# A two-layer decoder trunk on one core: the first chunk's inputs and weight pieces loaded and traced by turns, with identity products ahead of the data

## The chip, the cores and the metric

The kernel runs on one core of a Trainium2 chip. TensorE (PE in the profile) multiplies matrices, VectorE (DVE) and ScalarE (ACT) work element by element, GpSimd (POOL) does a few small operations, and SyncE (SP) issues the loads. Each engine has its own row of instructions and waits for others through semaphores. The metric is the time of one execution on the device in microseconds; a smaller number is better.

## The reference

An input of 256 tokens by 1024 channels goes through two layers. Each layer is a half-step SwiGLU feed-forward network, a token mixer (a causal convolution module in the first layer, a gated linear recurrence in the second) and another half-step feed-forward network, each between two RMS norms. The change lies in the very first feed-forward network:

```python
def rms_norm(x, gain):
    x32 = x.astype(jnp.float32)
    y = x32 * lax.rsqrt(jnp.mean(x32 * x32, axis=-1, keepdims=True) + EPS)
    return (y * gain.astype(jnp.float32)).astype(x.dtype)

def swiglu_ffn(x, w_in, w_out):
    gate, up = jnp.split(x @ w_in, 2, axis=-1)
    return (jax.nn.silu(gate) * up) @ w_out
...
    for layer in range(DEPTH):
        g = norm_gains[layer]
        h = swiglu_ffn(rms_norm(x, g[0]), ffn_w_in[layer, 0], ffn_w_out[layer, 0])
        x = x + 0.5 * rms_norm(h, g[1])
```

## The kernel before

The 256 tokens are two tiles of 128 (`xs[0]`, `xs[1]`). Every float32 operand is split into a high part (a cast on ACT, names `wh`, `xth`, `hid`) and a low part, the rest (a subtraction on DVE, names `wl`, `xtl`), and every product is three matmuls: high by high, high by low, low by high.

Weights come as pieces of 128 x 1024 floats, 512 KB each. `weight()` issues the load on SP into one of 4 `raw` buffers, and `split` makes `wh` on ACT and `wl` on DVE, of which there are 10 buffers each. With `fine` a piece is split in two halves. SP issues in order, and a load waits until DVE has read the piece that had its buffer. A chunk of a feed-forward network has 4 pieces of the first matrix and 2 of the second; a network has 11 chunks.

`pre_norm` transposes a tile of the input with the identity matrix on PE (L168), four blocks at a time into a `tr` buffer, scales them into `xth` on ACT (L172) and makes `xtl` on DVE (L178). In the first network `start` traces: tile 0's `pre_norm`, the four first pieces (`first_weights`), tile 1's `pre_norm`, then the means of squares (L156). `project_both` multiplies the first chunk for both tiles, 48 matmuls of 512 columns. `up` applies the gate to its result (L316 on ACT, L318 and L320 on DVE), and `turn` transposes that on PE (L189); from the second chunk on `channels` (L281 to L283) makes the products and `down` the second matrix (`acc`).

A scheduler orders each engine's instructions when the program is built. `tc.issue_after(i)` adds only this: what is traced inside stands behind `i` on `i`'s own engine. Behind chunk 2 `constants` is traced: `tap_spectrum` loads `dft` and the convolution's taps `w_dw` (31 rows of 4 KB), splits both, and multiplies them into `tr` buffers (the 31-row matmuls); `lower_bound` loads `logits`, `gnorm` and `masks`, and DVE casts the masks (L683).

Of the kernel before, what the change touches and what calls it, by code (L numbers as in the profile page):

```python
# [16 lines left out]
P = 128  # L17
# [23 lines left out]
def trunk_kernel(  # L41
# [62 lines left out]
    nc.sync.dma_start(xs[0][:, :512], x_in[0, :P, :512])  # L104
    nc.sync.dma_start(gcol, cols)
    nc.sync.dma_start(xs[0][:, 512:], x_in[0, :P, 512:])
    nc.sync.dma_start(xs[1], x_in[0, P:, :])
# [4 lines left out]
    last_hi = [None]  # L112
    last_split = [None]

    def weight(fine=False, eng=dve):
# [3 lines left out]
        nc.sync.dma_start(src, wts[n, :, half * 1024 : half * 1024 + 1024])  # L119
# [3 lines left out]
        with ExitStack() as held:  # L123
            if stream[0] <= 4:
                held.enter_context(tc.issue_after(last_hi[0]))
            for a in range(0, 1024, step):
                split(hi[:, a : a + step], lo[:, a : a + step], src[:, a : a + step], eng)
        return hi, lo

    def split(dst_h, dst_l, src, eng=dve):  # L130
        last_split[0] = act.copy(dst_h, src).ins  # L131
        eng.tensor_tensor(dst_l, src, dst_h.bitcast(F32), op=ALU.subtract)  # L132

    def mm3(o, lh, ll, rh, rl, first, last):
        pe.matmul(o, lh, rh, start=first, stop=False)  # L135
        pe.matmul(o, lh, rl, start=False, stop=False)  # L136
        pe.matmul(o, ll, rh, start=False, stop=last)  # L137
# [23 lines left out]
    def pre_norm(t, gi):  # L161
        src = xs[t]
        hi, lo = xth[:, t * D : (t + 1) * D], xtl[:, t * D : (t + 1) * D]
        for h in range(2):
            pt = tr()
            for j in range(4):
                k = h * 4 + j
                pe.transpose(pt[:, j * P : (j + 1) * P], src[:, k * P : (k + 1) * P], ident)  # L168
            for j in range(4):
                k = h * 4 + j  # L170
                g = gcol[:, gi * KD + k : gi * KD + k + 1]
                last_hi[0] = act.activation(hi[:, k * P : (k + 1) * P],  # L172
                                            pt[:, j * P : (j + 1) * P], AF.Copy, scale=g).ins
            for j in range(4):
                k = h * 4 + j
                g = gcol[:, gi * KD + k : gi * KD + k + 1]
                sl = slice(k * P, (k + 1) * P)
                dve.scalar_tensor_tensor(  # L178
                    lo[:, sl], pt[:, j * P : (j + 1) * P], g, hi[:, sl].bitcast(F32),
                    op0=ALU.mult, op1=ALU.subtract,  # L180
                )
# [648 lines left out]
```

## Time and profile before

| what | value |
|---|---|
| time, median of 3 runs | 1042.51 us (1040.93 to 1042.89) |
| span of the profiled execution, the only time the page gives of it | 1041.2 us |
| PE busy | 1011.2 us, 97% of the span |
| DVE busy | 707.1 us, 68% |
| ACT busy | 505.3 us, 49% |
| DMA, mean over the span | 174 GB/s |

The span runs from the first to the last instruction. A busy share is the part of the span in which an engine had an instruction running; the 3% in which PE did not are the places to look at.

### The profile page before, as it was taken

Reading aid. Unit: us, or ns where it says so; the run is one execution under the profiler, and the core shown is the slowest. Engines: PE = TensorE matmul, PEld = TensorE weight load, DVE = VectorE, ACT = ScalarE, POOL = GpSimd, SP = SyncE. Lnnn points to the kernel's source line nnn. Section 1 sums busy time; section 2 is a strip of 40 time slices with the busy share of each in tenths; the row PEclk is TensorE's granted clock in tenths of the full one; section 3 lists DMA queues with packets and bytes.
Section 4 is the critical chain, followed back from the end, with each engine's and each line's share of the span. In section 5 each row is a group of like instructions: output and inputs, shape, how many; then the busy total and the mean of one; then the engine's idle time right before and its main releaser. Section 6 shows DMA issues by size and latency. Waiting matters only on the chain. (4 is left out here: it accounts for less than half of the span.)

```text
span 1041.2 us, 16859 instructions
## 1 busy us (share of the span) xinstructions
PE 1011.2 (97%) x6676; PEld 920.0 (88%) x6676; DVE 707.1 (68%) x1088; ACT 505.3 (49%) x852; POOL 77.1 (7%) x120
## 2 busy tenths in 40 slices
PE   7989999999799999999999999999999999999997
PEld 6979999978678999999899999979888879999996
DVE  6845656699887657567856666686777686566663
ACT  7554444573575444445644445474133474444441
POOL 1000000010211000000100000021343010000000
PEclk9979999999899999999999999999999999999999
DMA  7744646664235646465546465555232545464641
GB/s 270 251 145 131 216 157 226 190 223 162 81 130 195 202 164 224 159 218 195 195 141 218 160 212 169 198 198 183 93 111 82 182 162 175 163 216 158 221 142 41
DMA packets 50510, 181.14 MB, mean 174 GB/s; under 512 B 5985, under 2 KB 6113, under 8 KB 50432
## 3 DMA queue, kind: packets, MB, share of 16 engines
q1 hardware_dynamic: 50432, 180.07, 51.8%
q8 instruction: 52, 0.85, 0.3%
q14 instruction: 26, 0.21, 0.1%
HBM read 179.00 MB, written 1.05 MB: 173 GB/s over the span
## 5 line engine op out<-in xcount | busy, mean ns | idle before, releaser
L132 DVE TENSOR_TENSOR wl<-raw,wh 128x1024 fp32r<-128x1024 f32 (+1 forms) x382 | 400.3, 1070 | 204.7 <-ACT wh L131 199.9
L131 ACT CAST wh<-raw 128x1024 fp32r<-128x1024 f32 (+1 forms) x386 | 336.6, 923 | 271.1 <-PE mm L282 131.3
L282 PE MATMUL mm<-xtl,wh 128*128 128x256 f32 x1408 | 397.8, 283 | 0.0
L281 PE MATMUL mm<-xth,wh 128*128 128x256 f32 x1408 | 397.5, 282 | 0.0
L283 PE MATMUL mm<-xth,wl 128*128 128x256 f32 x1408 | 397.4, 282 | 0.0
L281 PEld LDWEIGHTS mm<-xth,wh 128*128 128x128 f32 x1408 | 267.3, 190 | 2.9 <-issue 0.3
L282 PEld LDWEIGHTS mm<-xtl,wh 128*128 128x128 f32 x1408 | 266.5, 189 | 3.0 <-issue 0.3
L283 PEld LDWEIGHTS mm<-xth,wl 128*128 128x128 f32 x1408 | 267.5, 190 | 0.8 <-issue 0.3
L136 PE MATMUL acc<-wl,b 128*128 128x512 f32 x352 | 137.7, 391 | 0.0
L135 PE MATMUL acc<-wh,b 128*128 128x512 f32 x352 | 137.6, 391 | 0.0
L137 PE MATMUL acc<-wh,b 128*128 128x512 f32 x352 | 137.6, 391 | 0.0
L137 PEld LDWEIGHTS acc<-wh,b 128*128 128x128 f32 x352 | 66.1, 188 | 14.1
L136 PEld LDWEIGHTS acc<-wl,b 128*128 128x128 f32 x352 | 66.1, 188 | 11.4
L135 PEld LDWEIGHTS acc<-wh,b 128*128 128x128 f32 x352 | 66.1, 188 | 11.4
L334 ACT ACTIVATE e<-ga 128x256 f32<-128x256 f32 x80 | 33.4, 418 | 81.6 <-DVE ga L286 81.6
L242 PE MATMUL mm<-wh,xth 128*128 128x512 f32 x176 | 70.7, 402 | 0.0
L243 PE MATMUL mm<-wl,xth 128*128 128x512 f32 x176 | 70.1, 399 | 0.0
L286 DVE TENSOR_TENSOR ga<-mm,scales 128x512 f32<-128x512 f32 x88 | 60.3, 685 | 13.4 <-PE mm L283 13.3
L146 POOL TENSOR_SCALAR tiny<-tiny 128x1 f32<-128x1 f32 (+1 forms) x30 | 8.6, 288 | 808.9 <-ACT b L212 721.3
L131 ACT CAST b<-e 128x256 fp32r<-128x256 f32 x80 | 32.4, 405 | 52.4 <-DVE e L336 52.3
L246 PE MATMUL mm<-wh,xtl 128*128 128x512 f32 x176 | 49.8, 396 | 0.0
L132 DVE TENSOR_TENSOR b<-e,b 128x256 fp32r<-128x256 f32 x80 | 33.8, 423 | 21.3 <-ACT b L131 21.3
(157 smaller groups left out, 894.6 us busy)
## 6 DMA issues: line engine op xcount, KB each, us to landing
raw<-wts SPq DMA_DIRECT2D x328, 512.0 KB, 5.0
b<-rows SPq DMA_DIRECT2D x10, 512.0 KB, 6.2
out_dram<-x SPq DMA_DIRECT2D x4, 256.0 KB, 2.1
x<-x_in SPq DMA_DIRECT2D x2, 256.0 KB, 3.2
x<-x_in SPq DMA_DIRECT2D x1, 512.0 KB, 4.7
b<-dft SPq DMA_DIRECT2D x1, 371.0 KB, 6.0
ca<-masks SPq DMA_DIRECT2D x1, 192.0 KB, 6.9
b<-w_dw SPq DMA_DIRECT2D x1, 124.0 KB
```

The costliest lines, as they stand in the source:

```text
L131: last_split[0] = act.copy(dst_h, src).ins
L132: eng.tensor_tensor(dst_l, src, dst_h.bitcast(F32), op=ALU.subtract)
L135: pe.matmul(o, lh, rh, start=first, stop=False)
L136: pe.matmul(o, lh, rl, start=False, stop=False)
L137: pe.matmul(o, ll, rh, start=False, stop=last)
L242: pe.matmul(o, hi[:, kp], wh[:, sl], start=k == 0, stop=False)
L243: pe.matmul(o, hi[:, kp], wl[:, sl], start=False, stop=False)
L246: pe.matmul(o, a, w, start=False, stop=h == 1 and n == 3)
L281: pe.matmul(og, wh[:, cs], xkh[:, k], start=k == 0, stop=False)
L282: pe.matmul(og, wh[:, cs], xkl[:, k], start=False, stop=False)
L283: pe.matmul(og, wl[:, cs], xkh[:, k], start=False, stop=k == KD - 1)
L286: dve.tensor_tensor(pair(res), pair(o), scales.unsqueeze(1).broadcast_to([P, 2, SEQ]), op=ALU.mult)
```

## The change

The loads of the first chunk are issued by turns: half of tile 0, piece 0, the other half, piece 1, tile 1, pieces 2 and 3; the norm gains (`gcol`) are issued by ACT instead of SP. The body of `pre_norm` becomes `turn_x`, for one half of a tile. `boot` replaces `start` and `project_both` in the first network: it traces two groups of four identity products (`warm`, into a `tr` buffer that nobody reads), and then steps of three kinds by turns: transpose and scale half a tile, cast a piece, multiply. Each step is traced with `issue_after` the last ACT and the last PE instruction before it, so that ACT and PE take the steps in the written order. `lower_bound` now also stands behind the last piece's load on SP. The diff:

```diff
@@ -101,40 +101,39 @@
     xkh = xth.rearrange("p (t k m) -> p k t m", t=NT, m=P)
     xkl = xtl.rearrange("p (t k m) -> p k t m", t=NT, m=P)
     gcol = const.tile([P, G_END], F32, name="gcol")
-    nc.sync.dma_start(xs[0][:, :512], x_in[0, :P, :512])
-    nc.sync.dma_start(gcol, cols)
-    nc.sync.dma_start(xs[0][:, 512:], x_in[0, :P, 512:])
-    nc.sync.dma_start(xs[1], x_in[0, P:, :])
 
     stream = [0]
     ahead = []
     last_root = [None]
-    last_hi = [None]
-    last_split = [None]
-
-    def weight(fine=False, eng=dve):
+    last_act = [None]
+    last_pe = [None]
+    last_raw = [None]
+
+    def fetch_raw():
         n, half = divmod(stream[0], 2)
         stream[0] += 1
         src = new(sb, [P, 1024], F32, "raw", 4)
-        nc.sync.dma_start(src, wts[n, :, half * 1024 : half * 1024 + 1024])
+        last_raw[0] = nc.sync.dma_start(src, wts[n, :, half * 1024 : half * 1024 + 1024]).ins
+        return src
+
+    def weight(fine=False, eng=dve, src=None):
+        if src is None:
+            src = fetch_raw()
         hi = new(sb, [P, 1024], F32R, "wh", 10)
         lo = new(sb, [P, 1024], F32R, "wl", 10)
         step = 512 if fine else 1024
-        with ExitStack() as held:
-            if stream[0] <= 4:
-                held.enter_context(tc.issue_after(last_hi[0]))
-            for a in range(0, 1024, step):
-                split(hi[:, a : a + step], lo[:, a : a + step], src[:, a : a + step], eng)
+        for a in range(0, 1024, step):
+            split(hi[:, a : a + step], lo[:, a : a + step], src[:, a : a + step], eng)
         return hi, lo
 
     def split(dst_h, dst_l, src, eng=dve):
-        last_split[0] = act.copy(dst_h, src).ins
+        last_act[0] = act.copy(dst_h, src).ins
         eng.tensor_tensor(dst_l, src, dst_h.bitcast(F32), op=ALU.subtract)
 
     def mm3(o, lh, ll, rh, rl, first, last):
         pe.matmul(o, lh, rh, start=first, stop=False)
         pe.matmul(o, lh, rl, start=False, stop=False)
-        pe.matmul(o, ll, rh, start=False, stop=last)
+        last_pe[0] = pe.matmul(o, ll, rh, start=False, stop=last).ins
 
     def row(i):
         r = b4()
@@ -158,30 +157,78 @@
         pool.tensor_tensor(tot, ss[:, 0:1], ss[:, 1:2], op=ALU.add)
         return rsqrt(tot, 1.0 / D, EPS)
 
-    def pre_norm(t, gi):
+    def turn_x(t, gi, h):
         src = xs[t]
         hi, lo = xth[:, t * D : (t + 1) * D], xtl[:, t * D : (t + 1) * D]
+        pt = tr()
+        for j in range(4):
+            k = h * 4 + j
+            last_pe[0] = pe.transpose(pt[:, j * P : (j + 1) * P],
+                                      src[:, k * P : (k + 1) * P], ident).ins
+        for j in range(4):
+            k = h * 4 + j
+            g = gcol[:, gi * KD + k : gi * KD + k + 1]
+            last_act[0] = act.activation(hi[:, k * P : (k + 1) * P],
+                                         pt[:, j * P : (j + 1) * P], AF.Copy, scale=g).ins
+        for j in range(4):
+            k = h * 4 + j
+            g = gcol[:, gi * KD + k : gi * KD + k + 1]
+            sl = slice(k * P, (k + 1) * P)
+            dve.scalar_tensor_tensor(
+                lo[:, sl], pt[:, j * P : (j + 1) * P], g, hi[:, sl].bitcast(F32),
+                op0=ALU.mult, op1=ALU.subtract,
+            )
+        return hi, lo
+
+    def pre_norm(t, gi):
         for h in range(2):
-            pt = tr()
-            for j in range(4):
-                k = h * 4 + j
-                pe.transpose(pt[:, j * P : (j + 1) * P], src[:, k * P : (k + 1) * P], ident)
-            for j in range(4):
-                k = h * 4 + j
-                g = gcol[:, gi * KD + k : gi * KD + k + 1]
-                last_hi[0] = act.activation(hi[:, k * P : (k + 1) * P],
-                                            pt[:, j * P : (j + 1) * P], AF.Copy, scale=g).ins
-            for j in range(4):
-                k = h * 4 + j
-                g = gcol[:, gi * KD + k : gi * KD + k + 1]
-                sl = slice(k * P, (k + 1) * P)
-                dve.scalar_tensor_tensor(
-                    lo[:, sl], pt[:, j * P : (j + 1) * P], g, hi[:, sl].bitcast(F32),
-                    op0=ALU.mult, op1=ALU.subtract,
-                )
-        if gi == 0:
-            return hi, lo, None
-        return hi, lo, mean_square(src)
+            hi, lo = turn_x(t, gi, h)
+        return hi, lo, mean_square(xs[t])
+
+    def warm(n):
+        pt = tr()
+        for j in range(n):
+            sl = slice(j % 4 * P, (j % 4 + 1) * P)
+            last_pe[0] = pe.matmul(pt[:, sl], ident, ident, start=True, stop=True).ins
+
+    def boot():
+        act.dma_start(gcol, cols)
+        nc.sync.dma_start(xs[0][:, :512], x_in[0, :P, :512])
+        raws = [fetch_raw()]
+        nc.sync.dma_start(xs[0][:, 512:], x_in[0, :P, 512:])
+        raws += [fetch_raw()]
+        nc.sync.dma_start(xs[1], x_in[0, P:, :])
+        raws += [fetch_raw(), fetch_raw()]
+        xt, ws = {}, []
+
+        def turn(t, h):
+            xt[t] = turn_x(t, 0, h)
+
+        def cast():
+            ws.append(weight(True, src=raws[len(ws)]))
+
+        o = [mm(), mm()]
+
+        def multiply(t, i):
+            hi, lo = xt[t]
+            wh, wl = ws[i]
+            for k in (2 * i, 2 * i + 1):
+                sl = slice((k % 2) * 512, (k % 2) * 512 + 512)
+                kp = slice(k * P, (k + 1) * P)
+                mm3(o[t], hi[:, kp], lo[:, kp], wh[:, sl], wl[:, sl], k == 0, k == KD - 1)
+
+        warm(4)
+        turn(0, 0)
+        warm(4)
+        for step in (cast, lambda: multiply(0, 0), lambda: turn(0, 1), cast, lambda: multiply(0, 1),
+                     lambda: turn(1, 0), lambda: turn(1, 1), cast, cast,
+                     *(lambda t=t, i=i: multiply(t, i)
+                       for t, i in ((1, 0), (1, 1), (0, 2), (0, 3), (1, 2), (1, 3)))):
+            with tc.issue_after(last_act[0]), tc.issue_after(last_pe[0]):
+                step()
+        ahead.append(ws)
+        with tc.issue_after(last_act[0]):
+            return [(*xt[t], mean_square(xs[t])) for t in range(NT)], o
 
     def transposed(src, hi, lo, n, base, gain=None):
         pt = tr()
@@ -219,17 +266,6 @@
                 xs[t][:, sl], hg[:, sl], r, xs[t][:, sl], op0=ALU.mult, op1=ALU.add
             )
 
...
     def project(t, xt, ws):
         o = mm()
         hi, lo, _ = xt
@@ -290,15 +326,11 @@
     def start(gi, before):
         first = pre_norm(0, gi)
         before()
-        second = pre_norm(1, gi)
-        if gi == 0:
-            with tc.issue_after(last_split[0]):
-                return [(*first[:2], mean_square(xs[0])), (*second[:2], mean_square(xs[1]))]
-        return [first, second]
+        return [first, pre_norm(1, gi)]
 
     def ffn(layer, which, before, extra=None):
         base = layer * 3 + (0 if which == 0 else 2)
-        xt = start(base, before)
+        xt, o = boot() if before is None else (start(base, before), [None, None])
         accs = [None, None]
         w1, w2, hid, raw, both = {}, {}, {}, {}, {}
 
@@ -347,7 +379,6 @@
             expand(accs[t], hid.pop((t, c)), w2[c], c == 0, c == NC - 1)
 
         fetch(0)
-        o = project_both(xt, w1[0]) if extra is not None else [None, None]
         up(0, 0, o[0])
         up(1, 0, o[1])
         turn(0, 0)
@@ -708,12 +739,9 @@
 
     made = {}
 
-    def first_weights():
-        ahead.append([weight(True) for _ in range(4)])
-
     def constants():
         made["spectrum"] = tap_spectrum()
-        with tc.issue_after(last_split[0]):
+        with tc.issue_after(last_act[0]), tc.issue_after(last_raw[0]):
             made["lower"] = lower_bound()
 
     def store(t):
@@ -721,7 +749,7 @@
             sl = slice(n * 512, (n + 1) * 512)
             nc.sync.dma_start(out[0, t * P : (t + 1) * P, sl], xs[t][:, sl])
 
-    rest = ffn(0, 0, first_weights, constants)
+    rest = ffn(0, 0, None, constants)
     rest = conv_mixer(0, made["spectrum"], rest)
     rest = ffn(0, 1, rest)
     rest = ffn(1, 0, rest)
```

ACT's row at the start, before: four groups of `xth` for tile 0's two halves and tile 1's (named by the `tr` buffer read), and the casts of the first four pieces.

```order
L172 ACTIVATE xth<-tr_84,gcol 128x128 x4
L172 ACTIVATE xth<-tr_97,gcol 128x128 x4
L131 CAST wh_112<-raw_110 128x512 x2
L131 CAST wh_120<-raw_118 128x512 x2
L131 CAST wh_128<-raw_126 128x512 x2
L131 CAST wh_136<-raw_134 128x512 x2
L172 ACTIVATE xth<-tr_142,gcol 128x128 x4
L172 ACTIVATE xth<-tr_155,gcol 128x128 x4
```

The same stretch of ACT's row in the changed kernel:

```order
L171 ACTIVATE xth<-tr_99,gcol 128x128 x4
L130 CAST wh_117<-raw_82 128x512 x2
L171 ACTIVATE xth<-tr_129,gcol 128x128 x4
L130 CAST wh_142<-raw_85 128x512 x2
L171 ACTIVATE xth<-tr_154,gcol 128x128 x4
L171 ACTIVATE xth<-tr_167,gcol 128x128 x4
L130 CAST wh_180<-raw_88 128x512 x2
L130 CAST wh_186<-raw_90 128x512 x2
```

The casts of pieces 1, 2 and 3 now stand behind evictions of transposes. PE's row at the start of the changed kernel, where `tr_94` and `tr_112` are the identity products and `mm_92` is tile 0's product:

```order
L192 MATMUL tr_94<-ident 128x128 x4
L166 MATMUL tr_99<-ident,x_75 128x128 x4
L192 MATMUL tr_112<-ident 128x128 x4
L134 MATMUL mm_92<-wh_117,xth 128x512
L135 MATMUL mm_92<-wl_118,xth 128x512
L136 MATMUL mm_92<-wh_117,xtl 128x512
L134 MATMUL mm_92<-wh_117,xth 128x512
L135 MATMUL mm_92<-wl_118,xth 128x512
L136 MATMUL mm_92<-wh_117,xtl 128x512
L166 MATMUL tr_129<-ident,x_75 128x128 x4
L134 MATMUL mm_92<-wh_142,xth 128x512
```

Before, the transposes of tile 0's second half and of tile 1's first stood ahead of the first product, and those of tile 1's second half right behind it; now six products stand ahead of tile 0's second half, and tile 1's transposes stand behind all twelve of pieces 0 and 1.

The third place is PE's row at the end of the last `acc` product ahead of the taps' products. Before:

```order
L137 MATMUL acc_466<-wh_323,b_66_329 128x512
L135 MATMUL tr_668<-b_109_662,b_106_656 81x256
L135 MATMUL tr_676<-b_109_662,b_106_656 81x256
L281 MATMUL mm_766<-xth,wh_731 128x256
L136 MATMUL tr_668<-b_110_663,b_106_656 81x256
```

And in the changed kernel:

```order
L136 MATMUL acc_476<-wh_333,b_68_339 128x512
L317 MATMUL mm_776<-xth,wh_741 128x256
L318 MATMUL mm_776<-xtl,wh_741 128x256
L319 MATMUL mm_776<-xth,wl_742 128x256
L317 MATMUL mm_776<-xth,wh_741 128x256
L318 MATMUL mm_776<-xtl,wh_741 128x256
L319 MATMUL mm_776<-xth,wl_742 128x256
L317 MATMUL mm_776<-xth,wh_747 128x256
L134 MATMUL tr_678<-b_111_672,b_108_666 81x256
L134 MATMUL tr_686<-b_111_672,b_108_666 81x256
```

Seven products of the next chunk now stand ahead of the first product of the taps.

## Rows read from the trace of the kernel before

**Rows 1.** Two lines of the page: the span, and PE's busy time with its share of the span and its instructions.

```profile
span 1041.2 us, 16859 instructions
...
PE 1011.2 (97%) x6676; PEld 920.0 (88%) x6676; DVE 707.1 (68%) x1088; ACT 505.3 (49%) x852; POOL 77.1 (7%) x120
```

**Rows 2.** The longest waits of PE over the whole span: what waited, for which engine and line; us in total, times, longest.

```profile
PE tr L135 <- ACT cc L131: 5.6, 1, 5.6
PE tr L168 <- DMA x<-x_in: 4.7, 3, 3.3
PE tr L135 <- ACT b L131: 4.5, 1, 4.5
```

**Rows 3.** ACT in order of time at the start: start, length of the merged group, line, operation, output <- input, shape, count, and in brackets the idle time ahead with what ended it.

```profile
4.47 1.15 ACT L172 ACTIVATE xth<-tr,gcol 128x128 fp32r<-128x128 f32 x4 [2.25 <-PE tr L168]
...
8.15 1.14 ACT L131 CAST wh<-raw 128x512 fp32r<-128x512 f32 x2 [0.93 <-DMA raw<-wts]
...
13.22 2.17 ACT L172 ACTIVATE xth<-tr,gcol 128x128 fp32r<-128x128 f32 x8
15.24 0.67 ACT L156 ACTIVATE b<-x 128x512 f32<-128x512 f32 x1
...
20.52 0.48 ACT L316 ACTIVATE e<-mm,tiny 128x256 f32<-128x256 f32 x1 [0.62 <-PE mm L137]
```

**Rows 4.** DVE in order of time at the start, same columns.

```profile
5.65 1.13 DVE L178 SCALAR_TENSOR_TENSOR xtl<-tr,gcol,xth 128x128 fp32r<-128x128 f32 x4 [5.65 <-ACT xth L172]
...
8.80 5.32 DVE L132 TENSOR_TENSOR wl<-raw,wh 128x512 fp32r<-128x512 f32 x8 [0.42 <-ACT wh L131]
...
22.15 0.48 DVE L320 SCALAR_TENSOR_TENSOR e<-mm,tiny,e 128x256 f32<-128x256 f32 x1
```

**Rows 5.** PE in order of time, from the first transpose to the first instruction behind the 48 products of the first chunk, same columns.

```profile
3.35 1.09 PE L168 MATMUL tr<-ident,x 128*128 128x128 f32 x4 [3.35 <-DMA x<-x_in]
...
8.82 0.79 PE L135 MATMUL mm<-wh,xth 128*128 128x512 f32 x1 [0.80 <-ACT wh L131]
9.42 1.05 PE L168 MATMUL tr<-ident,x 128*128 128x128 f32 x4
...
11.12 0.63 PE L135 MATMUL mm<-wh,xth 128*128 128x512 f32 x1
11.55 0.63 PE L136 MATMUL mm<-wl,xth 128*128 128x512 f32 x1
...
14.66 0.39 PE L135 MATMUL mm<-wh,xth 128*128 128x512 f32 x1
14.89 0.40 PE L136 MATMUL mm<-wl,xth 128*128 128x512 f32 x1
...
23.06 0.38 PE L189 MATMUL tr<-ident,e 128*128 128x128 f32 x2
```

**Rows 6.** DMA issues of the first 4.5 us: output <- input, queue, count, KB each, median us from issue to landing.

```profile
raw<-wts SPq DMA_DIRECT2D x4, 512.0 KB, 6.8
x<-x_in SPq DMA_DIRECT2D x2, 256.0 KB, 3.2
x<-x_in SPq DMA_DIRECT2D x1, 512.0 KB, 4.7
```

**Rows 7.** The timeline of all engines from 50 to 64 us, the rows around the taps' products; SPq is SP's queue of issues.

```profile
50.36 0.43 SPq L691 DMA_DIRECT2D b<-dft  x1
...
50.85 0.33 SPq L695 DMA_DIRECT2D b<-w_dw  x1
...
56.40 0.81 ACT L131 CAST b<-b 128x742 fp32r<-128x742 f32 x1 [3.98 <-DMA b<-dft]
...
57.12 2.94 ACT L131 CAST wh<-raw 128x1024 fp32r<-128x1024 f32 x3
...
57.78 0.39 PE L137 MATMUL acc<-wh,b 128*128 128x512 f32 x1
...
61.62 1.04 ACT L131 CAST b<-b 31x1024 fp32r<-31x1024 f32 x1 [1.56 <-DMA b<-w_dw]
...
62.72 0.71 PE L135 MATMUL tr<-b,b 31*81 31x256 f32 x2 [4.55 <-ACT b L131]
```

**Rows 8.** DVE in order of time ahead of that: a cast of the masks, and the low parts of the last pieces ahead of `dft` and `w_dw` in SP's queue.

```profile
37.77 1.09 DVE L683 CAST msk<-ca 128x512 uint8<-128x512 f32 x3
...
45.06 0.42 DVE L336 TENSOR_TENSOR e<-e,ga 128x256 f32<-128x256 f32 x1
46.04 1.23 DVE L132 TENSOR_TENSOR wl<-raw,wh 128x1024 fp32r<-128x1024 f32 x1 [0.56 <-ACT wh L131]
...
48.73 1.23 DVE L132 TENSOR_TENSOR wl<-raw,wh 128x1024 fp32r<-128x1024 f32 x1 [1.12 <-ACT wh L131]
```

**Rows 9.** Stretches of the trace: from and to, length, busy time (and instructions) of PE, weight loads, DVE, ACT, POOL, then the granted share of TensorE's clock, the DMA engines' busy share, GB/s.

```profile
58.00:60.00 2.00, 0.17 (x1) 0.00 (x0) 1.98 (x3) 2.00 (x3) 0.00 (x0) 1.00 0.06 27
...
62.00:64.00 2.00, 1.26 (x4) 0.67 (x4) 1.30 (x2) 1.97 (x3) 0.00 (x0) 0.52 0.72 248
...
74.00:76.00 2.00, 2.00 (x13) 2.00 (x12) 1.54 (x2) 0.10 (x1) 0.00 (x0) 0.57 0.26 66
76.00:78.00 2.00, 2.00 (x19) 2.00 (x18) 0.00 (x0) 0.00 (x0) 0.00 (x0) 1.00 0.89 322
...
281.00:283.00 2.00, 2.00 (x11) 2.00 (x10) 2.00 (x6) 2.00 (x7) 0.00 (x0) 0.50 0.02 6
```

## What was predicted

> **What bounds the kernel now.** I read the page first: PE is busy for 97% of a span of 1041.2 us [rows 1], so whatever delays PE's row by a microsecond at the start moves the end by about as much, unless a later wait of PE swallows it. So I read PE's waits next. The longest are three [rows 2]: 5.6 us in the convolution, 4.7 us for the input at the start, and 4.5 us at the first product of the taps. Then I read the three engines through the first 23 us. The first product starts at 8.82 us; from 9.42 us on PE hardly pauses, and the 48 products of the first chunk are behind it at 23.06 us [rows 5]. Up to about 14 us products follow each other every 0.43 us (11.12, 11.55), later every 0.23 us (14.66, 14.89) [rows 5]: by that spacing PE runs at the lower of its two levels (1.2 GHz) and then at the upper one (2.4 GHz).
>
> Before 23.06 us ACT is nearly as loaded as PE. It evicts tile 0, casts four pieces as they land, evicts tile 1 without a pause (2.17 us for eight blocks), takes the squares from 15.24 us, and applies the first gate at 20.52 us after a pause of only 0.62 us [rows 3].
>
> The last stretch I read is the wait at the taps. The load of `w_dw` is issued at 50.85 us and its cast waits for it until 61.62 us; PE is through at about 58.2 us and idles 4.55 us, until 62.72 [rows 7]. Behind that wait PE's granted clock is 0.5 and comes back between 74 and 76 us [rows 9]: some 13 us at half clock, a loss of about 6.5 us. So that place costs 11 us, and what the change does there matters as much as the start.
>
> **The change, part by part.** *Loads.* Piece 0 stands second in SP's queue. The first half of x takes 3.2 us to land, the pieces 6.8 at the median [rows 6]. ACT is not free for the first cast before 4.47 + 1.15 = 5.62 us [rows 3], and by the bytes ahead of it the piece (0.75 MB in all) should land between 4.5 us (its neighbours' pace) and 5.8. The first product then moves from 8.82 to 5.62 + 0.6 = 6.3 us. The gains' load on ACT costs nothing: ACT waits 2.25 us before its first eviction [rows 3].
>
> *Identity products.* Four fit between the identity and 3.35 us, when the input is there; four more lie in the wait between 4.44 and 6.3 us. They cost nothing as long as those waits are there; without them four cost about as much as four transposes, 1.1 us [rows 5]. What they may do is to the clock, see below.
>
> *The order.* Here I follow the new rows with the old durations. An eviction of four blocks takes 1.15 us on ACT, then 1.13 on DVE, which starts when ACT has done all four (5.65 after 4.47 + 1.15) [rows 3, 4]; a cast in two halves takes 1.14, its first half 0.6 [rows 3]; a low half takes DVE 5.32 / 8 = 0.66 [rows 4].
> Piece 0: DVE is free at 5.65 + 1.13 = 6.8 and has the first low half at 7.4. The second product starts then; six end, at 0.43 each, at 9.6 us. Only now come the transposes of tile 0's second half (1.05 us [rows 5]), until 10.6; ACT evicts until 11.8 and casts half of piece 1 by 12.4, although that piece landed long before; DVE has the low part of x at 12.95 and the first low half at 13.6. Six products end at 13.6 + 5 x 0.43 = 15.8 us. Then tile 1's transposes: the first four end at 16.8, ACT evicts eight blocks in 2.17 us until 19.0 and casts pieces 2 and 3 in another 2.2 us until 21.1. Before, the four casts ran from 8.15 us on and were all done when tile 1's evictions began at 13.22 [rows 3].
> From here ACT's row is the old one. From the squares to the first gate it needs 20.52 - 15.24 - 0.62 = 4.66 us [rows 3], so the gate comes at 25.8, and from its start to the end of DVE's second gate product 22.63 - 20.52 = 2.1 us pass [rows 3, 4]: 27.9 us. PE needs that for the transposes that started at 23.06. So they start **4.8 us later**.
> PE itself: the third product of tile 1 waits for DVE until 18.3 us, and 34 are left. At the upper level all the way that is 18.3 + 34 x 0.233 = 26.2; with the lower level until 21 it is 27.6. Both lie under ACT's 27.9, so I take 4.8. The bounds come from the clock. At the upper level from the first product on, six products take 1.4 us instead of 2.6 and the transposes half, the whole chain shortens by some 3 us, and the delay is 1.8. If the lower level lasts until 24 us, PE is the last at 28.9 and the delay is 5.9.
> The pieces of the next chunk are late by the same amount: their buffers come free with the low parts of pieces 2 and 3, at 21.4 and 22.6 us, and with those of the two pieces cast behind the squares. So both PE and the stream of loads carry the delay on.
>
> *The order and the skill.* The row: ACT's casts at 57.12 us stood behind the cast of `dft`, which waited 3.98 us for its load [rows 7]. The Trainium skill, "TensorE: Matmul & The Clock Gate", section "Architectural detail", says of ScalarE and VectorE that they take instructions strictly first in, first out. If ACT could pass a waiting eviction, the casts would start at landing and PE's 26.2 would be the later end, a delay of 3.1 instead of 4.8 and 1045.4 us in all; the trace agrees with the page.
>
> *The constants.* The loads of `logits`, `gnorm` and `masks` move from ahead of the fifth piece to behind chunk 2's, and DVE's six mask casts (1.09 / 3 = 0.36 each [rows 8]) with their small companions, about 2.5 us, now stand in one block behind the product at 45.06 us. The low part that started at 46.04 then starts some 2 us later, and the next one, which had waited 1.12 us for its cast and started at 48.73, about 0.6 later [rows 8]. That one frees the buffer of the last piece ahead of `dft` and `w_dw`, so `w_dw` lands **0.6 us later** (between 0, if the earlier casts' going frees as much as this takes, and 2).
>
> *Seven products* of the next chunk now stand ahead of the taps' first. They run in what was PE's wait, half as many columns as those at 0.233, so **0.8 us less** is left behind it. The wait itself stays: PE gets there 0.8 later, the taps 0.6 later, 4.4 us instead of 4.55, at the same place of the pieces' stream. So I keep the half clock behind it.
>
> Sum: 4.8 + 0.6 - 0.8 = 4.6 us on a span of 1041.2, hence 1045.8; the span is 1.3 us under the median of the runs, 1042.51, so the time is **1047.1 us**.
>
> **The rivals.** *No half clock behind the taps.* What is new is that PE's wait there is 4.4 instead of 4.55 us, or shorter if PE is more delayed than the stream of loads. Waits of 4.5 and 5.6 us are the two longest in the middle of the span [rows 2], and half clock follows them [rows 9]; no wait between 1 and 4.5 us is there to show where that begins. If the wait falls under that point, 6.5 us come back: 1047.1 - 6.5 = 1040.6, or 1039 with a shorter wait. This is the one that ends on the other side; it decides from a wait some tenths shorter than the old one at the earliest.
> *An early clock.* The identity products bring the upper level by about 11 us and PE keeps it: the second half of tile 0 and tile 1 come 1.5 us sooner, 4.6 - 1.5 = 3.1, 1045.6; from the first product on 4.6 - 3 = 1.6, 1044.1. For it: eight more products by 6 us. Against it: PE still waits at 10.6 to 12.4 and 12.9 to 13.6.
> *The lower level lasts longer*, until 24 us or once more behind the taps: 5.9 instead of 4.8, or 1.7 us more at half clock: 1048 to 1050.5. The Trainium skill, same page, "Part 4: PE-mode transpose", says that transposes do not count as busy for the clock. The trace agrees as far as it goes: the transposes at 3.35 and 9.42 us did not bring the upper level, which came only after 11.55 us, among the products [rows 5]. With the page the time would be this rival's.
> *The change does what it says*: the first product 2.5 us earlier and everything after it too, 1042.5 - 2.5 = 1040.0. It needs ACT to deliver piece 1 by 9.6 us, and its row has the eviction in between.
>
> **How the numbers follow.** My forecast, 1044.7 to 1048: 0.50. Lower level longer, 1048 to 1050.5: 0.13. Early clock, 1043.5 to 1045.7: 0.15, of which a third under 1044.6. No half clock behind the taps: 0.15, two thirds under 1040.4. The change as it says: 0.07, half under 1040.4. A measurement of this kernel tells 0.2%, 2.1 us, from no change. Faster: 0.10 + 0.035 = 0.14. Same (1040.4 to 1044.6): 0.05 + 0.05 + 0.035 = 0.14. Slower: 0.72. The range must reach to the half-clock case to leave out no more than 0.2: 1040.5 to 1050; the likeliest case alone is 1044.7 to 1048.
>
> **What would show it.** Right: the first product near 6.3 us, PE waiting near 10.6 and 13 us, the cast of piece 1 not before 11.7, the last casts of the first four pieces near 21, the first transposes of the gate's result near 28, PE's wait at the taps near 4.4 us with half clock behind it. Wrong: pieces 2 and 3 cast by 17 us, products at 0.23 us spacing by 11 us, or a granted clock of 1.00 from 65 to 80 us; the last alone makes the kernel as fast as before or faster.

## The result and the profile after

The changed kernel takes 1050.02 us (median of 4 runs, 1048.48 to 1050.50), the kernel before 1042.67 beside it: a ratio of 1.0069, with a 95% interval of 1.0056 to 1.0083. It is slower by 7.3 us. The prediction said slower, 1047.1; the median lies at the upper end of its range (1040.5 to 1050), 2 us above its likeliest case (1044.7 to 1048). The page of the profiled execution, its span and PE's line:

```profile
span 1048.7 us, 16889 instructions
...
PE 1016.1 (97%) x6692; PEld 923.5 (88%) x6692; DVE 706.0 (67%) x1088; ACT 505.3 (48%) x852; POOL 77.0 (7%) x120
```

The span is 7.5 us longer than in [rows 1]; PE is busy for 4.9 us more of it, more than the 3.8 us of the two groups of identity products (2.1 and 1.7). So some products took longer, and I read both the waits and the clock. The longest waits of PE (us in total, times, longest):

```profile
PE tr L134 <- ACT b L130: 5.8, 1, 5.8
PE tr L134 <- ACT cc L130: 5.6, 1, 5.6
...
PE mm L134 <- ACT wh L130: 2.4, 2, 1.7
...
PE tr L236 <- DVE e L352: 1.3, 1, 1.3
```

The wait for the input is gone from this list [rows 2], two waits of the turns are new (`wh`, `e`), and the wait at the taps grew from 4.5 to 5.8. ACT at the start, in order of time, with the idle time ahead and what ended it:

```profile
4.77 1.14 ACT L171 ACTIVATE xth<-tr,gcol 128x128 fp32r<-128x128 f32 x4 [2.12 <-PE tr L166]
6.23 1.14 ACT L130 CAST wh<-raw 128x512 fp32r<-128x512 f32 x2 [0.32 <-DMA raw<-wts]
9.63 1.14 ACT L171 ACTIVATE xth<-tr,gcol 128x128 fp32r<-128x128 f32 x4 [2.26 <-PE tr L166]
10.65 1.15 ACT L130 CAST wh<-raw 128x512 fp32r<-128x512 f32 x2
15.84 2.18 ACT L171 ACTIVATE xth<-tr,gcol 128x128 fp32r<-128x128 f32 x8 [4.04 <-PE tr L166]
17.86 2.23 ACT L130 CAST wh<-raw 128x512 fp32r<-128x512 f32 x4
...
24.47 0.51 ACT L348 ACTIVATE e<-mm,tiny 128x256 f32<-128x256 f32 x1
```

ACT waits for PE's transposes for 2.26 and 4.04 us, while in [rows 3] it waited mostly for loads. PE over the same stretch:

```profile
6.90 0.49 PE L134 MATMUL mm<-wh,xth 128*128 128x512 f32 x1 [0.64 <-ACT wh L130]
...
8.53 0.40 PE L135 MATMUL mm<-wl,xth 128*128 128x512 f32 x1
8.76 0.40 PE L136 MATMUL mm<-wh,xtl 128*128 128x512 f32 x1
9.00 0.60 PE L166 MATMUL tr<-ident,x 128*128 128x128 f32 x4
11.34 0.49 PE L134 MATMUL mm<-wh,xth 128*128 128x512 f32 x1 [1.74 <-ACT wh L130]
12.59 0.66 PE L135 MATMUL mm<-wl,xth 128*128 128x512 f32 x1 [0.76 <-DVE wl L131]
...
13.47 0.63 PE L134 MATMUL mm<-wh,xth 128*128 128x512 f32 x1
13.90 0.63 PE L135 MATMUL mm<-wl,xth 128*128 128x512 f32 x1
...
14.75 1.74 PE L166 MATMUL tr<-ident,x 128*128 128x128 f32 x8
...
26.94 0.44 PE L236 MATMUL tr<-ident,e 128*128 128x128 f32 x2 [1.31 <-DVE e L352]
```

The first six products follow each other at 0.23 us, the upper level, as early as 8.5 us; then PE waits twice, and at 13.5 us they stand 0.43 apart. The gate's transposes start at 26.94 instead of 23.06 [rows 5]: 3.9 us late.

The taps (SP's issues, then DVE, ACT and PE); the first raw piece shown is the one ahead of the moved constants:

```profile
42.31 0.33 SPq L116 DMA_DIRECT2D raw<-wts  x1
42.68 0.43 SPq L691 DMA_DIRECT2D logits<-logits  x1
...
57.47 0.42 SPq L722 DMA_DIRECT2D b<-dft  x1
...
53.36 1.43 DVE L714 CAST msk<-ca 128x512 uint8<-128x512 f32 x4
54.70 2.35 DVE L131 TENSOR_TENSOR wl<-raw,wh 128x1024 fp32r<-128x1024 f32 x2
...
63.43 0.81 ACT L130 CAST b<-b 128x742 fp32r<-128x742 f32 x1 [3.90 <-DMA b<-dft]
...
69.78 0.71 PE L134 MATMUL tr<-b,b 31*81 31x256 f32 x2 [5.82 <-ACT b L130]
```

`dft` is issued 7.1 us later than in [rows 7], the taps' first product 7.06. Stretches, with the granted clock third from the end:

```profile
6.00:8.00 2.00, 1.03 (x5) 0.53 (x4) 2.00 (x6) 1.14 (x2) 0.00 (x0) 1.00 0.89 313
...
14.00:16.00 2.00, 2.00 (x9) 1.70 (x8) 0.00 (x0) 0.16 (x1) 0.00 (x0) 0.50 0.76 254
...
84.00:86.00 2.00, 2.00 (x12) 1.78 (x12) 0.69 (x1) 0.29 (x1) 0.00 (x0) 0.89 0.00 0
...
290.00:292.00 2.00, 2.00 (x9) 1.81 (x9) 0.91 (x3) 2.00 (x6) 0.00 (x0) 0.50 0.00 0
```

The upper level is there at 5.9 us, lost again between 12.8 and 16.2, and the half clock behind the taps lasts until 84.5: 14.7 us from the taps' first product, 13.0 before [rows 9]. The clock column has to be read with care at the start: up to the first change on record it shows 1.00 at either level. In the kernel before it does so from 11 to 12 us, while products stand 0.43 us apart [rows 5]; so up to that first change I go by the spacing of products. The second half-clock stretch (at 281 us before) lasts 10.2 us instead of 6.8. It lasts 10.2 us in the profiles of all twelve other kernels below as well, so the short one is that one execution of the kernel before, and the difference is not shown to come from the change.

PE's delay against the kernel before at the same instruction: 3.9 us at the gate's transposes, 4.4 behind them (a product waits 0.3 us for the cast of `hid`), 5.0 from 49 us on (times of the kernel before; one product waits for a cast on ACT, another for a low part that DVE makes behind two casts of the masks), 7.1 at the taps' first product, 6.95 at 80 us, 7.75 behind the second stretch of half clock, 7.5 at the end.

### The profile page after: what moved, and what is told of

It reads as the page before. It is cut to its first block, busy times and chain, and to the rows that moved or that the text cites. A ratio compares the mean times of both kernels' runs of the same rounds, so it can differ in the third digit from the quotient of the medians.

```text
span 1048.7 us, 16889 instructions
## 1 busy us (share of the span) xinstructions
PE 1016.1 (97%) x6692; PEld 923.5 (88%) x6692; DVE 706.0 (67%) x1088; ACT 505.3 (48%) x852; POOL 77.0 (7%) x120
## 4 chain that ended last, share of the span: by engine, by line
PE 85%; DVE 6%; DMA 4%; ACT 3%; POOL 1%; issue 1%; SPq 0%; DVEq 0%; POOLq 0%; ACTq 0%
PE mm L318 15%; PE mm L317 15%; PE mm L319 15%; PE acc L135 7%; PE acc L136 7%; PE acc L134 7%; PE mm L282 3%; PE mm L278 3%; PE mm L279 3%; DMA raw<-wts 3%; PE tr L595 2%; DVE wl L131 2%; PE tr L166 1%; DMA b<-w_dw 1%; ACT b L259 1%
## 5 line engine op out<-in xcount | busy, mean ns | idle before, releaser
L135 PEld LDWEIGHTS acc<-wl,b 128*128 128x128 f32 x352 | 66.1, 188 | 11.4
L322 DVE TENSOR_TENSOR ga<-mm,scales 128x512 f32<-128x512 f32 x88 | 60.2, 684 | 16.7 <-PE mm L319 16.6
```

The source lines that it names most:

```text
L322: dve.tensor_tensor(pair(res), pair(o), scales.unsqueeze(1).broadcast_to([P, 2, SEQ]), op=ALU.mult)
```

## The experiments

Three questions. Is it the order of the turns that costs the start, or the loads? Is it the moved constants that cost 2 us on the way to the taps? And what do the identity products do? **The theory:** the turns make ACT wait for transposes that stand behind products; the constants hold up the stream of loads; the clock gains at the start and loses in the waits. **The rival:** the loads by turns land too late for any order, and the delay at the taps is only the start's, handed on.

All results, as ratios to the kernel before on the same chip; the last two columns are from the profiled execution, us:

| run | ratio (95%) | gate's transposes | PE's wait at the taps |
|---|---|---|---|
| before | 1 | 23.06 | 4.55 |
| changed | 1.0069 (1.0056 to 1.0083) | 26.94 | 5.82 |
| free_order | 1.0051 (1.0034 to 1.0067) | 26.99 | 5.89 |
| old_order | 0.9984 (0.9969 to 0.9998) | 23.93 | 4.56 |
| turns_ahead | 1.0018 (1.0006 to 1.0030) | 22.87 | 3.36 |
| constants_early | 1.0074 (1.0057 to 1.0091) | 31.72 | 2.41 |
| consts_late_only | 1.0018 (1.0006 to 1.0030) | 23.85 | 5.52 |
| no_identity | 1.0077 (1.0061 to 1.0094) | 28.30 | 5.93 |
| identity_only | 0.9987 (0.9976 to 0.9998) | 23.42 | 2.76 |
| taps_early | 0.9959 (0.9947 to 0.9970) | 23.79 | 2.0, among them |
| two_loads | 0.9984 (0.9971 to 0.9998) | 23.16 | 4.41 |
| ahead_taps | 0.9934 (0.9918 to 0.9949) | 23.14 | 1.85, among them |
| ahead_sq_taps | 0.9903 (0.9888 to 0.9919) | 22.58 | none |
| ahead_no_id | 0.9928 (0.9916 to 0.9940) | 23.15 | none |

The last two columns come from one execution each. before, two_loads and taps_early have the same start, and their gate's transposes stand at 23.06, 23.16 and 23.79: a difference of under some 0.7 us there shows nothing.

**The rule alone taken away.**

```diff
-            with tc.issue_after(last_act[0]), tc.issue_after(last_pe[0]):
-                step()
+            step()
```

> The changed kernel without the rule that holds ACT and PE to the written order; the loads by turns, the identity products and the late constants stay. Order theory: the delay at the start (3.9 us at the first transposes of the gate's result) goes, the delay at the taps (2.1 us) stays, so 1044 to 1046 us against 1050. Rival, the loads by turns or the identity products cost it: the transposes of the gate's result start no sooner than 26 us and the time stays at 1049 to 1051.

The order theory, put like this, failed: 26.99 us, as late as with the rule, and 1048.89 us in all. ACT and PE show why:

```profile
10.97 1.14 ACT L130 CAST wh<-raw 128x512 fp32r<-128x512 f32 x2 [1.41 <-DMA raw<-wts]
12.01 1.14 ACT L171 ACTIVATE xth<-tr,gcol 128x128 fp32r<-128x128 f32 x4
```

```profile
12.43 0.79 PE L134 MATMUL mm<-wh,xth 128*128 128x512 f32 x1 [5.37 <-ACT xth L171]
```

Without the rule the scheduler does not go back to the old order. It puts the casts of three pieces ahead of the first eviction, and the third waits for its load until 10.97; the first product starts at 12.43, 5.5 us later than with the rule. So the rule is not the cause; the sequence it holds may still be. That needs the old sequence, held by the same rule.

**The old sequence and the new loads; and the new sequence with transposes one step ahead.**

```diff
 # old_order
+        for step in (lambda: turn(0, 1), cast, cast, cast, cast, lambda: turn(1, 0),
+                     lambda: multiply(0, 0), lambda: turn(1, 1), lambda: multiply(0, 1),
...
 # turns_ahead
+        for step in (cast, lambda: turn(0, 1), lambda: multiply(0, 0), cast, lambda: turn(1, 0),
+                     lambda: multiply(0, 1), lambda: turn(1, 1), cast, cast,
...
```

> The changed kernel (loads by turns, identity products, late constants, the rule that holds the order), with the steps written in the order of the kernel before: both halves of tile 0, the four casts, then tile 1, with the transposes ahead of the products. If the 3.9 us come from the order in which the steps are written: the gate's transposes start at 23 to 24.3 us (26.9 in the changed kernel, 23.06 before), and with the delay at the taps left in, 1044.5 to 1046.5 us. Rival, the loads by turns land too late for any order: 26 us or later, 1048 or more.

> The changed kernel with one thing moved: each half tile's transposes stand one multiply step further ahead in PE's row (and the eviction ahead of the next cast on ACT), all other steps as changed. If it is the transposes behind the products that make ACT's row late: no wait of PE over 1 us between 7 and 16 us, the casts of pieces 2 and 3 done by 16 us (19.9 in the changed kernel), the gate's transposes at 21.5 to 23.5 us, 1043 to 1045.5 us in all. Rival, the loads: waits for x and the pieces take their place, 25 us or later, 1047.5 or more.

With the same loads, identity products and rule, the old sequence brings the gate's transposes back to 23.93 and the time to 0.9984 of the kernel before. The rival on the loads falls. In turns_ahead (PE):

```profile
9.72 0.66 PE L166 MATMUL tr<-ident,x 128*128 128x128 f32 x4 [0.41 <-DMA x<-x_in]
...
12.17 0.60 PE L166 MATMUL tr<-ident,x 128*128 128x128 f32 x4
...
22.87 0.44 PE L236 MATMUL tr<-ident,e 128*128 128x128 f32 x2 [1.46 <-DVE e L352]
```

Moving each half tile's transposes one multiply step ahead takes 4.1 us off the start (26.94 to 22.87); tile 1's transposes come at 9.72 and 12.17 instead of 14.75, and ACT has cast all four pieces by 16.0. One expected point missed: PE still waits 1.25 us for `x`, at 7.28. Both sequences confirm the place of the transposes as the cause of the start's delay. old_order came out below its range (1042.82 us), although it has the late constants too: in its profile the start is 0.9 us late, the taps 1.8, and 1.2 us are left at 80 us. Which of the two is the better one stays open: the profiled executions say turns_ahead (span 1041.5 against 1042.7), the medians say old_order.

**The constants, from both sides.**

```diff
 # constants_early: the changed kernel
-        with tc.issue_after(last_act[0]), tc.issue_after(last_raw[0]):
+        with tc.issue_after(last_act[0]):
 # consts_late_only: the kernel before
-        with tc.issue_after(last_split[0]):
+        with tc.issue_after(last_split[0]), tc.issue_after(last_raw[0]):
```

> The changed kernel with the loads of logits, gains and masks back ahead of the fifth piece, all else as changed. Constants theory: the 2.1 us that the taps' products lost between 58 and 70 us come back and the half clock behind them gets shorter, so 1046.5 to 1048.5; the first product of the taps starts near 67.7 us. Rival, that delay is only the start's, handed on and grown: 1049.5 to 1050.5, first product of the taps at 69.5 or later.

> The kernel before with one part of the change alone: the constants' loads behind the last piece of chunk 2 on SP. Constants theory: the first product of the taps starts 2 us later (64.5 to 65.5 us instead of 62.72), the time is 1044 to 1046. Rival, as in the prediction's sum: 0.6 us later, 1043.0 to 1043.5. Third: without the delay at the start there is room for the masks' casts and nothing changes, 1042.3 to 1042.8.

What to read is the time from SP's issue of the last piece ahead of the late constants to that of `dft`, six pieces further. Before, constants_early, consts_late_only, one fence each:

```profile
37.55 0.33 SPq L119 DMA_DIRECT2D raw<-wts  x1
```

```profile
46.75 0.33 SPq L116 DMA_DIRECT2D raw<-wts  x1
...
59.40 0.43 SPq L722 DMA_DIRECT2D b<-dft  x1
```

```profile
38.48 0.33 SPq L120 DMA_DIRECT2D raw<-wts  x1
...
53.09 0.42 SPq L692 DMA_DIRECT2D b<-dft  x1
```

50.36 [rows 7] - 37.55 = 12.81 us before and 12.65 with early constants; 14.61 with late ones alone and 57.47 - 42.31 = 15.16 in the changed kernel. So the two pairs that differ in this edit alone give 1.8 and 2.5 us that the late constants cost the stream of loads. The other kernels with `dft` at the old place bear it out: 14.7 to 15.9 us in four with late constants, 11.4 and 13.0 in two with early ones. In consts_late_only the taps' first product comes at 65.29, 2.6 us later, 0.8 of which is a later start, and the time grows by 0.18%: the constants theory's size at the taps, not the 0.6 us of the sum.

turns_ahead, which keeps the late constants and loses the late start, stands at 1.0018 too. By the ratios, then, the order makes 0.51% (5.3 us) of the changed kernel's 0.69% and the constants 0.18% (1.9 us). old_order does not fit this division: it has the late constants and is at 0.9984. Why is open.

But constants_early gained nothing. Its taps' first product, at 69.54, and its time, 1051.72 us, lie where its rival had them or above, yet not for the rival's reason: its start is 4.8 us later still, and 31.72 us shows what the late constants save in this order. DVE, then PE:

```profile
13.43 2.10 DVE L714 CAST msk<-ca 128x512 uint8<-128x512 f32 x6 [5.17 <-DMA ca<-masks]
15.44 1.12 DVE L177 SCALAR_TENSOR_TENSOR xtl<-tr,gcol,xth 128x128 fp32r<-128x128 f32 x4
```

```profile
17.22 0.79 PE L135 MATMUL mm<-wl,xth 128*128 128x512 f32 x1 [5.41 <-DVE wl L131]
```

The six mask casts stand ahead of tile 0's second low part in DVE's row and wait for their load until 13.43; PE waits 5.4 us behind them. So the edit that costs 2 us later saves 4.8 at the start of the same kernel. In this run PE's wait at the taps is 2.41, and its delay there 6.8, less than the 9.0 it came with: the delay of the start is not handed on in full, let alone grown.

**The identity products.** In no_identity the two `warm(4)` are taken out of the changed kernel; in identity_only they are added to the kernel before, ahead of tile 0's transposes.

> The changed kernel without the eight identity products. Clock theory: they brought the upper level by 5.94 us and saved some time in the first six products and the transposes of tile 0's second half; without them the products at the start stand 0.43 us apart until behind 14 us, the gate's transposes start at 28 us or later (26.9 with them), and the time is 1051 to 1053. Rival, they are only work in front of the transposes (0.27 us): 1049.5 to 1050.

> The kernel before with one part of the change alone: four identity products ahead of each of tile 0's two groups of transposes. Clock theory: the upper level comes at about 6 us (14.3 before) and stays, because nothing here makes PE wait as the turns do; the products at the start stand 0.23 us apart from the first on, but ACT's evictions and casts then set the pace, so 1 to 1.5 us of the possible 2.2 arrive: 1041 to 1042 us. Rival, PE's rows at the start are set by ACT alone: 1042.3 to 1043.

Without them, PE and then a stretch, with the granted clock third from the end:

```profile
8.72 0.63 PE L134 MATMUL mm<-wh,xth 128*128 128x512 f32 x1
9.14 0.63 PE L135 MATMUL mm<-wl,xth 128*128 128x512 f32 x1
...
12.70 0.50 PE L134 MATMUL mm<-wh,xth 128*128 128x512 f32 x1 [1.74 <-ACT wh L130]
```

```profile
14.00:16.00 2.00, 2.00 (x5) 1.52 (x6) 0.50 (x1) 0.00 (x0) 0.00 (x0) 0.54 0.22 68
```

The products there stand 0.43 us apart (8.72, 9.14). The upper level comes at 10.7 us instead of 5.9, earlier than the 14 us expected, and is lost again from 14.2 to 17.6; the gate's transposes come at 28.30 instead of 26.94. So the identity products are worth 1.4 us at the start of these two executions; the ratios (1.0077 and 1.0069) point the same way, but their intervals overlap. In the old kernel they raise the clock at 6.6 us, it falls again at 10.0 while PE waits 1.89 us for the first cast, and returns at 13.4: only 0.13% faster (0.9976 to 0.9998, which just leaves out 1). The rival was right about the start, where nothing was gained (23.42). What was gained lies at the taps, where `w_dw` landed earlier than in [rows 7]; why it did is open.

**The taps.**

```diff
 # two_loads: the kernel before
-        nc.sync.dma_start(taps[:W_CONV], w_dw)
+        nc.sync.dma_start(taps[:16], w_dw[:16])
+        nc.sync.dma_start(taps[16:W_CONV], w_dw[16:])
 # taps_early: these two loads and dft's, traced in chunk 1 (behind 17 pieces on SP instead of 24)
```

> The kernel before with one edit: the 31 rows of the taps loaded as 16 and 15. If the 1.56 us that ACT waits for the taps' load come from one DMA engine moving 31 rows one after the other, the load lands before ACT gets there, PE's wait falls from 4.55 to about 3 us, the clock still falls behind it: 1040.5 to 1041.5. Rival, the load waits for its place behind the pieces, however it is cut: 4.3 to 4.6 us, 1042.3 to 1043.

> The kernel before with the loads of the taps and of their matrix traced one chunk earlier (and the 31 rows in two loads). Theory that the 4.55 us wait and the half clock behind it are both that load's: the wait falls under 1.5 us, the granted clock stays 1.0 behind it, 1031.5 to 1036 us. Rival one, the wait goes but the half clock stays or comes elsewhere: 1037 to 1040. Rival two, the pieces behind these loads become as late as the taps were, and PE waits for them instead: 1041 to 1043.

In two_loads ACT casts the taps without a wait; the 1.56 us of [rows 7] are gone, the first half of the expectation:

```profile
62.98 1.03 ACT L131 CAST b<-b 31x1024 fp32r<-31x1024 f32 x1
```

PE's wait stayed at 4.41, because `dft` was issued 1.6 us later in this run and the casts of four pieces stood between; the time is 0.16% shorter. So the slow load was real, but something else would have been late. The Trainium skill, "DMA: Bandwidth & Descriptors", section "Why a DMA increments its semaphore by 16 and not by 1", says that a load runs on the largest number of engines, up to 16, that divides the slowest dimension of both its sides, here the 31 rows; that leaves one. The trace of the kernel before agrees: from 58 to 60 us the engines' busy share was 0.06, one of 16 [rows 9].

taps_early does what the first theory said of the wait, not of the clock: the taps' products start at 58.83 with no wait ahead of them, a wait of 2.0 us comes in their middle, and half clock lasts for 10.2 us (62.4 to 72.7) in its place. That is rival one, 3.9 us gained at that place (the delay goes from 0.7 to -3.2) and 1039.04 us in all.

**Together.**

> Both edits together: the changed kernel with the transposes one step ahead, and the taps' loads traced one chunk earlier. If the two places are independent, the start stays at the old kernel's (gate's transposes at 22.9 us) and the taps give what they gave alone, some 3.5 to 4 us: 1038 to 1039.5. Rival, the gain at the taps was a shift within the stream of loads that the late masks and logits take again: a wait of over 3 us at the taps and 1041 to 1044.

> The same, and the squares of tile 0 on ACT moved from behind the casts to the pause ahead of tile 1's second eviction. PE's last wait at the start (1.46 us for the gate on DVE) should shrink by 0.9 to 1.5 us: the gate's transposes at 21.4 to 22 us, 1037 to 1038.5. Rival, the casts of the next pieces still stand ahead of the gate on ACT and it starts no earlier than 20.2: no more than 0.3 us better than without.

> The last kernel (transposes one step ahead, squares ahead, taps' loads early) without the eight identity products. If they still matter when PE hardly waits at the start: the upper level comes behind 13 us instead of 10.8, and the gate's transposes start 0.7 to 1.5 us later, 1034.5 to 1035.5 us. Rival, ACT's row sets the start now and takes up the difference: the gate's transposes within 0.4 us of 22.58, 1033.5 to 1034.3.

```diff
 # ahead_sq_taps: ahead_taps, and one step more
+                     lambda: roots.append(mean_square(xs[0])),
                      lambda: multiply(0, 1), lambda: turn(1, 1), cast, cast,
```

The third is the second without identity products. ahead_taps came out better than the two gains together (1037.34 us): its half clock at the taps lasts 6.8 us (63.8 to 70.6), 10.2 in taps_early. In ahead_sq_taps PE's row at the gate shows:

```profile
22.58 0.44 PE L238 MATMUL tr<-ident,e 128*128 128x128 f32 x2 [0.38 <-DVE e L354]
```

The wait for the gate shrank by 1.1 us as expected, but the gate's transposes came only 0.56 us earlier, which is within the spread of that instant; the clock came later in this execution (10.8 us, 9.2 in ahead_taps). The larger gain is the half clock behind the taps, down to 3.4 us (62.0 to 65.4), with no pause of PE ahead of it or among the taps' products:

```profile
62.00:64.00 2.00, 2.00 (x11) 1.70 (x10) 1.34 (x2) 1.75 (x4) 0.00 (x0) 0.51 0.87 279
...
66.00:68.00 2.00, 2.00 (x19) 2.00 (x18) 0.00 (x0) 0.00 (x0) 0.00 (x0) 1.00 0.81 268
```

1033.89 us, 0.97% faster than the kernel before: the best version here, and faster than both kernels. Without the identity products it takes 1035.65; the gate's transposes come 0.57 us later, between the two expectations, and the clock at 12.7. The intervals overlap a little and the profiled executions say the opposite (spans 1033.5 with them, 1032.3 without), so whether they still pay here is not shown.

## Why the prediction came out as it did

The direction and the mechanism at the start came out; the size did not, 4.6 us foretold on the span and 7.5 measured. That the wide range still reaches to the result is luck: the time lies where the *lower level lasts longer* rival put it, of which one half came (1.7 us more of half clock behind the taps) and the other did not (the clock is at 1.00 from 16.2 us on, not from 24).

**The turns, right; a little too dear.** The first product came at 6.90 (6.3 foretold, its cast waited 0.3 us for the load), PE waited ahead of 11.34 and 12.59 (10.6 to 12.4 and 12.9 to 13.6), the last casts ended at 20.1 (21.1), the gate's transposes started at 26.94 (27.9): 3.9 us instead of 4.8. In no_identity, whose first products stand 0.43 us apart as in the sum, it is 28.30, 5.2 us late, so like for like the sum was 0.4 too small. turns_ahead shows that the named mechanism, transposes behind products, is the cause.

**The clock at the start, wrong in the step that held 0.43 us for the first six products.** They ran at 0.23 us. This is the *early clock* rival's first half; its second half failed as its "against" said, since the level fell in PE's waits. Against no_identity it gave back 1.4 us, which is how 4.8 came out as 3.9.

**The identity products, free as the sum had them, though dearer in themselves.** The sum priced four at 1.1 us, by the transposes, where no wait hides them. Each leaves two records 0.21 us apart, and the first four run from 1.49 to 3.57 us, 2.1 us. The input's transposes start at 3.62, 0.27 us later than in [rows 5], but that is the load: in no_identity, with nothing ahead of them, they start at 3.61 behind a wait for `x`.

**Pauses behind the start, left out:** 0.5 us at once, with the wait for `hid`, and 0.6 at 49 us, together 1.1.

**The constants, the term that was mis-sized:** 0.6 in the sum, bounds 0 and 2. Measured, 2.1 at PE (7.06 - 4.96) and 1.8 and 2.5 in the loads. The step that failed is the slack: the sum let the low part of 46.04 start 2 us late and the next only 0.6, because that one had waited for its cast [rows 8]. After, DVE goes from the masks straight into both low parts (54.70, x2); the slack was gone, and the second one, which frees `dft`'s predecessor, moved by 2.7 us beyond the start's 4.4.

**The seven products, right:** PE's delay at 80 us is 0.1 us below that at the taps' first product, although the half clock from there lasts 1.7 us longer, which costs half of that, 0.8.

**The wait at the taps, wrong:** 5.82 instead of 4.4, the late constants less the products. The *no half clock* rival needed far more than some tenths: taps_early and ahead_taps show half clock around waits of 2.0 and 1.85 us, and of the two kernels in which PE does not pause there at all, ahead_sq_taps still has 3.4 us of it and only ahead_no_id keeps 1.00, from 12.7 to 265 us.

**Half clock taken as unchanged, wrong by 0.8 us behind the taps.** The longer wait came with a longer half clock: 17.1 us of it around the taps in the four kernels that wait 5.5 us or more there, 13.7 before and in three others with waits of 2.8 to 4.6; two_loads, with 4.41, is the exception (6.8 us and another 3.4). Another 0.8 lies in the second stretch, but that is the short stretch of the one execution before, not a term that the sum missed.

Sum: start 3.9, pauses 1.1, constants 2.1, from the taps to 80 us -0.1, second stretch 0.8, later -0.2: 7.5 us (rounded terms sum to 7.6), against 4.6 foretold. Of the 2.9 us missed, 1.5 are the constants, 1.6 the clock's later stretches (0.8 of it not shown to be the change's) and 1.1 the pauses; the start took 0.9 off and the rest 0.4.

## What to carry to other kernels

When work is ordered by turns, put the producer of the next turn (here the transposes) one step ahead of the consumer of this one, on the engine that does both; the order as written cost 3.9 us, and the moved one none (26.94 and 22.87 against 23.06 us). An edit that takes a load out of an early queue pays where it goes: look at what the later place releases, and count slack there as gone once the row has been moved. Taking a constraint away is not undoing an order: the scheduler's own order may be a third one. And before a difference between two profiles is put down to a change, look at the same place in the profiles of other kernels: the second stretch of half clock was the odd one in the kernel before.

## What the runs showed of the hardware

In five of the kernels with two groups of four 128x128 products of the identity, begun at 1.49 us, the granted clock was at 1.0 by 5.4 to 6.6 us (without them 14.0 to 15.0 in the old order, 10.7 and 12.7 in the new ones). In ahead_taps and ahead_sq_taps it came at 9.2 and 10.8, and in free_order, where PE waited 5.4 us behind them, at 16.7. It did not last through waits of 1.7 us (changed), 1.9 (identity_only) or 2.5 (old_order); in turns_ahead, whose longest wait there was 1.25 us, it did.

In ahead_sq_taps half clock came without a wait: PE was busy throughout, with the taps' products of 31 rows and 256 columns. In ahead_no_id the same products ran at 1.00.

Executions of one kernel differ by some microseconds, and the clock tells only part of it. In turns_ahead a span of 1045.2 us had a mean granted clock of 0.984 and one of 1039.2 had 0.989; 0.005 of 1045 is 5.2 of those 6.0 us. In the kernel before, one of 1039.9 us had 0.987 and one of 1043.5 had 0.989. So a difference of a microsecond in one profiled execution says little about the median.
